# Last MLP of a hybrid decoder trunk: low parts of the weights made by an accumulating DMA onto the negated high parts, where VectorE subtracted

## The chip, the core and the metric

The kernel runs on one core of one Trainium2 chip. The time is device microseconds (us) for one execution of the whole program; a figure for a kernel is the median of several runs. The engines are named as in the profile: PE (TensorE matmuls), PEld (its weight loads), DVE (VectorE), ACT (ScalarE), POOL (GpSimd), SP (SyncE, which here only issues DMAs).

## What is computed

Two decoder layers on 528 tokens (16 learned meta tokens and 512 real ones) of width 1024, all in float32. Layer 0 is an mLSTM group beside an RG-LRU group, layer 1 is differential attention, and after each comes an MLP:

```python
def _sq_relu_mlp(hn, w1, w2):
    a = jax.nn.relu(hn @ w1)          # w1: 1024 x 4096
    return (a * a) @ w2               # w2: 4096 x 1024
...
        h = h + _sq_relu_mlp(_rmsnorm(h, norm_mlp[layer]), mlp_w1[layer], mlp_w2[layer])
    h = _rmsnorm(h, norm_final)
    return h[:, N_META:, :]
```

The change concerns the second of these MLPs, the last stage of the program.

## The kernel before

**Split products.** Matmuls run in float32r. To keep float32 accuracy every operand is split in two: a high part, which is the float32r rounding of the value, and a low part, which is the value minus its high part. A product is then three matmuls: high x high, high x low, low x high. For a weight tile `raw` the high part `wh` is made by a copy with conversion on ACT (L169) and the low part `wl = raw - wh` by a subtraction, usually on DVE (L117, the helper `sub`, called from L177).

**Units.** All weights are cut into 225 units of 128x1024 float32 (512 KB), used in a fixed order. `emit_load` (L150 to L179) prepares one unit: SP issues the load of `raw` (L162), ACT makes `wh`, DVE or POOL makes `wl`. `get_w` (L203) is called where a unit is used and first emits loads up to two units ahead. `unit_mm` (L210) then runs one unit: eight blocks k, and in each the three matmuls `wh`x high, `wh`x low, `wl`x high (L220). In the last MLP a matmul has 512 columns, so a unit is 24 matmuls, and `wl` is first read by the third of them.

**Buffers.** `raw` has two buffers (pool `wr`), `wh` and `wl` three each (pool `wp`). So the load of unit i+2 has to wait until everything that reads `raw` of unit i is done, and the copy that makes `wh` of unit i has to wait until PE has finished with unit i-3. The last eight units (indices 217 to 224) have eight buffers of their own for `wh` and `wl` (tag `wf`), and so are prepared ahead of their use.

**The last MLP.** It holds the unit indices 161 to 224: four quarters of 16 units, eight of w1 ("up") and eight of w2 ("down"). After an up unit DVE applies the relu and the norm's factor (L692), ACT squares (L694), ACT and DVE split the result (L120 and L117). After a down unit DVE adds the product to `h` (L705). The last eight units are the w2 of the fourth quarter; `final_quarter` takes them all at once, turned around so that tokens lie on the partitions, and goes through them eight times for four blocks of tokens: for the first block with k outermost, so unit 224 is needed last. The final norm and the output follow.

**Who makes the low parts.** A set `POOL_L` gives eight unit indices to POOL, 161 and 164 among them in the last MLP; all other low parts there are DVE's. Units 129 to 160 were split earlier in the program and are only loaded.

**Order.** Instructions of each engine stand in a fixed order, made by a scheduler from the order in the code and from priorities: what stands under `soon()` (the copy and the subtraction of a unit among it) is drawn forward.

Of the kernel before, what the change touches and what calls it, by code (L numbers as in the profile page):

```python
# [10 lines left out]
F32 = mybir.dt.float32  # L11
F32R = mybir.dt.float32r
AF = mybir.ActivationFunctionType
ALU = mybir.AluOpType
# [39 lines left out]
POOL_OPS = "Mm"  # L54

POOL_L = {5, 33, 43, 44, 52, 126, 161, 164}
N_S = 31

AHEAD = range(129, 161)
# [23 lines left out]
def trunk(tc, hT, wu, wri, pk, lv, rope, gf, out, probe=None):  # L83
    nc = tc.nc
# [6 lines left out]
    with ctx:  # L91
# [14 lines left out]
        def sc(name, dt=F32, w=T):  # L106

            return big.tile([P, T], dt, tag="s", name=name, bufs=N_S)

# [6 lines left out]
        def sub(eng, o, a, b):  # L116
            eng.tensor_tensor(out=o, in0=a, in1=b, op=ALU.subtract)  # L117
# [19 lines left out]
        def soon():  # L137
            return tc.high_priority(offset=BOOST)
# [12 lines left out]
        def emit_load():  # L151
            i = state["next"]
            u = seq[i]
            if i in AHEAD:
                wh, wl = (wp.tile([P, 1024], F32R, tag="w" + p, name=f"w{p}{i}") for p in "hl")
                for w, part in zip((wh, wl), parts[i - AHEAD[0]]):
                    nc.sync.dma_start(out=w.bitcast(F32), in_=part)
                ready.append((wh, wl))
                state["next"] += 1
                return  # L160
            raw = wr.tile([P, 1024], F32, tag="raw", name=f"raw{i}")
            nc.sync.dma_start(out=raw, in_=wu[u])  # L162
            if u >= N_UNIT - 8:
                wh, wl = (wp.tile([P, 1024], F32R, tag="wf" + p, name=f"w{p}{i}", bufs=8) for p in "hl")
            else:
                wh = wp.tile([P, 1024], F32R, tag="wh", name=f"wh{i}")
                wl = None if u == U_GATE else wp.tile([P, 1024], F32R, tag="wl", name=f"wl{i}")
            with soon():
                nc.scalar.copy(wh, raw)  # L169
                eng = nc.gpsimd if i in POOL_L else nc.vector  # L170
                if u == U_GATE:

                    hi, r = (a.rearrange("p (k c) -> p k c", k=KB) for a in (wh, raw))
                    sub(eng, hi[:, :, 64:100], r[:, :, 0:36], hi[:, :, 0:36].bitcast(F32))
                else:
                    sub(eng, wl, raw, wh.bitcast(F32))
            ready.append((wh, wl))  # L177
            state["next"] += 1
# [21 lines left out]
        def get_w(u):  # L200
            while state["next"] <= min(state["use"] + 2, len(seq) - 1):
                emit_load()
            assert seq[state["use"]] == u  # L203
            state["use"] += 1
            return ready.pop(0)
# [100 lines left out]

        h0 = big.tile([P, KB, T], F32, tag="h", name="h0")
        emit_load()
        for k in range(KB):
            nc.sync.dma_start(out=h0[:, k, :], in_=hT[:, k, :])  # L310
            if k == LOAD1:
                emit_load()
# [781 lines left out]
```

## Time and profile before

| | before |
|---|---|
| median of 3 runs | 1462.95 us (1461.53 to 1465.24) |
| the profiled execution, its own time | 1463.24 us |
| its span, first to last instruction | 1461.4 us |
| PE busy | 1437.9 us, 98% of the span |
| DVE busy | 814.5 us, 56% |
| ACT busy | 650.8 us, 45% |
| POOL busy | 214.0 us, 15% |
| granted TensorE clock | 0.999 |

The profile is of one execution. Its times are counted from the span's start. The views used below are: the page's summary of engines and its slices; busy time by stretch; groups of instructions by line; the table of waits (who waited for whom, total, times, longest); the list of DMA issues with sizes and the time from issue to landing; and the list of instructions in order of time, in which a row has the start, the duration, the engine, the line, the operation and its tiles, and in brackets how long the engine had been idle and what released it.

### The profile page before, as it was taken

How to read it: one execution, taken by the hardware profiler on the slowest of the kernel's cores; microseconds unless marked ns; L12 is line 12 of the kernel's file. 1: busy time of each engine (PE TensorE's matmuls, PEld its weight loads, DVE VectorE, ACT ScalarE, POOL GpSimd, SP SyncE). 2: the span in 40 equal slices, each digit the busy share in tenths (PEclk: the TensorE clock that was granted, in tenths of full speed). 3: DMA queues.
4: the chain of work that ended last, by engine and by line, in shares of the span. 5: the costliest groups of instructions: out<-in, count | busy, mean ns of one | idle time of the engine just before them, and what ended most of it. 6: DMA issues, size and time to landing. Idle time of an engine off the chain costs nothing. (4 is left out here: it accounts for less than half of the span.)

```text
span 1461.4 us, 24650 instructions
## 1 busy us (share of the span) xinstructions
PE 1437.9 (98%) x9970; PEld 1338.6 (92%) x9970; DVE 814.5 (56%) x1423; ACT 650.8 (45%) x1154; POOL 214.0 (15%) x286
## 2 busy tenths in 40 slices
PE   8999999999999999999999999999999999999998
PEld 8999999999999999999999998989887888888886
DVE  6867754667544545545445568777755344343452
ACT  6454743647334424334334536565644223142342
POOL 4000001010012231322314511101031000000001
PEclk9999999999999999999999999999999999999999
DMA  7332224231223685857857875555332332333331
GB/s 255 98 116 80 89 72 133 60 101 59 88 87 102 217 272 175 266 183 234 283 180 245 297 230 156 170 158 181 124 116 88 100 91 97 98 90 101 89 126 46
DMA packets 70046, 210.11 MB, mean 144 GB/s; under 512 B 13066, under 2 KB 14615, under 8 KB 69932
## 3 DMA queue, kind: packets, MB, share of 16 engines
q1 hardware_dynamic: 53996, 157.15, 34.4%
q0 software_dynamic: 15360, 50.34, 10.4%
q8 instruction: 78, 1.28, 0.4%
q10 hardware_dynamic: 576, 1.05, 0.2%
q14 instruction: 36, 0.29, 0.1%
HBM read 162.11 MB, written 35.71 MB: 135 GB/s over the span
## 5 line engine op out<-in xcount | busy, mean ns | idle before, releaser
L169 ACT CAST wh<-raw 128x1024 fp32r<-128x1024 f32 x193 | 202.6, 1050 | 503.7 <-PE mm L220 402.8
L117 DVE TENSOR_TENSOR wl<-raw,wh 128x1024 fp32r<-128x1024 f32 x184 | 227.1, 1235 | 66.9 <-ACT wh L169 66.5
L705 DVE TENSOR_TENSOR h<-mm,h 128x264 f32<-128x264 f32 (+1 forms) x88 | 41.2, 498 | 109.8 <-PE mm L220 109.8
L117 DVE TENSOR_TENSOR ral<-ra,rah 128x512 fp32r<-128x512 f32 x64 | 43.7, 688 | 56.4 <-ACT rah L120 56.4
L120 ACT CAST rah<-ra 128x512 fp32r<-128x512 f32 x64 | 39.5, 617 | 69.3 <-DMA ra<-wu 69.1
L692 DVE SCALAR_TENSOR_TENSOR rt<-mm,mrstd 128x264 f32<-128x264 f32 x64 | 24.7, 428 | 76.7 <-PE mm L220 76.7
L692 DVE SCALAR_TENSOR_TENSOR rt<-mm,nrstd 128x512 f32<-128x512 f32 x32 | 22.1, 692 | 79.2 <-PE mm L220 79.1
L273 POOL TENSOR_TENSOR nsq<-nsq 128x528 f32<-128x528 f32 (+1 forms) x28 | 46.2, 1652 | 93.1 <-ACT nsq L271 87.8
L982 POOL TENSOR_TENSOR zg<-z,gfr 128x512 f32<-128x512 f32 x4 | 5.2, 1296 | 342.0 <-DVE z L980 336.2
L785 POOL TENSOR_TENSOR qr<-qr,tb 128x512 f32<-128x512 f32 (+1 forms) x16 | 24.6, 1536 | 166.5 <-DVE qs L784 159.1
L117 POOL TENSOR_TENSOR wl<-raw,wh 128x1024 fp32r<-128x1024 f32 x8 | 19.2, 2403 | 201.6 <-ACT wh L169 120.4
L853 ACT ACTIVATE e<-psc,mx 128x264 f32<-128x264 f32 (+3 forms) x80 | 38.2, 482 | 9.1 <-DVE mx L846 8.1
L846 DVE TENSOR_REDUCE mx<-psc 128x1 f32<-128x264 f32 (+3 forms) x80 | 33.2, 430 | 15.5 <-PE psc L844 7.8
L694 ACT ACTIVATE rt<-rt 128x528 f32<-128x528 f32 (+1 forms) x64 | 40.6, 636 | 2.8 <-DVE rt L692 2.8
L197 POOL DMA_DIRECT2D ra<-wu x64 | 34.7, 547 | 2.9 <-issue 2.9
L663 DVE TENSOR_TENSOR h<-mm,h 128x264 f32<-128x264 f32 x32 | 12.2, 426 | 38.0 <-PE mm L220 38.0
L120 ACT CAST rh<-qr 128x512 fp32r<-128x512 f32 (+1 forms) x16 | 10.0, 627 | 51.2 <-DVE qr L787 48.2
L365 POOL TENSOR_SCALAR_AFFINE_SELECT cb<-cb 128x128 f32<-128x128 f32 (+2 forms) x20 | 7.7, 397 | 166.3 <-DMA cb<-crow 166.1
L886 ACT CAST pp<-pt 128x128 fp32r<-128x128 f32 (+2 forms) x64 | 21.0, 342 | 16.4 <-PE pt L874 14.4
L220 PE MATMUL mm<-ax0h,wh 128*128 128x264 f32 x98 | 22.0, 297 | 6.3 <-ACT ax0h L262 6.3
L840 PE MATMUL psc<-st,st 128*128 128x264 f32 (+3 forms) x80 | 26.4, 331 | 1.3 <-ACT e L853 0.9
L117 DVE TENSOR_TENSOR pp<-pt,pp 128x128 fp32r<-128x128 f32 (+2 forms) x64 | 23.8, 382 | 3.6 <-ACT pp L886 3.5
(866 smaller groups left out, 4908.7 us busy)
## 6 DMA issues: line engine op xcount, KB each, us to landing
raw<-wu SPq DMA_DIRECT2D x193, 512.0 KB
ra<-wu POOLq DMA_DIRECT2D x64, 256.0 KB, 5.0
h<-hT SPq DMA_DIRECT2D x16, 264.0 KB
st<-rh SPq DMA_DIRECT2D x32, 132.0 KB
kz<-rl SPq DMA_DIRECT2D x16, 132.0 KB
st<-rh SPq DMA_DIRECT2D x16, 128.0 KB
st<-rl SPq DMA_DIRECT2D x16, 128.0 KB
cb<-crow SPq DMA_DIRECT2D x4, 264.0 KB
```

The source lines that it names most:

```text
L117: eng.tensor_tensor(out=o, in0=a, in1=b, op=ALU.subtract)
L120: nc.scalar.copy(hl[0][:, sl], src)
L169: nc.scalar.copy(wh, raw)
L197: nc.gpsimd.dma_start(out=raw, in_=wu[seq[i]][:, c])
L273: nc.gpsimd.tensor_tensor(out=fin[0][:, lo:], in0=fin[0][:, lo:], in1=sq[:, lo:], op=ALU.add)
L692: nc.vector.scalar_tensor_tensor(out=t[:, tk], in0=p, scalar=0.0, in1=rs[:, tk], op0=ALU.max, op1=ALU.mult)
L694: nc.scalar.activation(out=t[:, lo:], in_=t[:, lo:], func=AF.Square)
L705: nc.vector.tensor_tensor(out=h[:, c, tk], in0=p, in1=h[:, c, tk], op=ALU.add)
L785: pool_or_dve("mM"[w]).tensor_tensor(out=raw[:, lo:], in0=raw[:, lo:], in1=tb[0][:, lo:], op=ALU.mult)
L840: nc.tensor.matmul(d[:, :m], qS[c][:, qs], kS[c][:, s0:s0 + m], start=True, stop=False)
L846: nc.vector.tensor_reduce(out=mx[:, 2 * c + r:2 * c + r + 1], in_=d[:, :m], axis=AX.X, op=ALU.max, negate=True)
L853: nc.scalar.activation(out=e[:, s0:s0 + m], in_=d[:, :m], func=AF.Exp, bias=mx[:, 2 * c:2 * c + 1], accum_out=ss[:, c + 2 * r:c + 2 * r + 1])
```

## The change

For the unit indices 165 to 216, 52 units of the last MLP, the low part is made in another way. ACT, which has just written `wh`, writes `-wh` into the `wl` tile (a second ACT pass over 128x1024), and then POOL issues a DMA that reads `raw` and adds it to what stands in `wl`. The subtraction on DVE is left out for these units. Units 161 and 164 stay with POOL, 162 and 163 with DVE, and the last eight, 217 to 224, with DVE. The numbers are the same, since `raw + (-wh)` is `raw - wh`.

```diff
 POOL_L = {5, 33, 43, 44, 52, 126, 161, 164}
+
+DMA_L = range(165, 217)
 N_S = 31
...
             with soon():
                 nc.scalar.copy(wh, raw)
+                if i in DMA_L:
+
+                    nc.scalar.activation(out=wl, in_=wh.bitcast(F32), func=AF.Copy, scale=-1.0)
+                    nc.gpsimd.dma_start(out=wl.bitcast(F32), in_=raw, accum_op=ALU.add)
                 eng = nc.gpsimd if i in POOL_L else nc.vector
                 if u == U_GATE:
...
-                else:
+                elif i not in DMA_L:
                     sub(eng, wl, raw, wh.bitcast(F32))
```

The line numbers of the changed kernel are higher by 2 at the helpers (L117 becomes L119, L120 becomes L122, L169 becomes L171) and by 6 behind `emit_load` (L694 becomes L700); the new lines are L174 (the negation) and L175 (the DMA).

On ACT, in the first up quarter of the last MLP, these rows stood before (a copy of a weight unit, the square and the copy of an activation):

```order
L169 CAST wh_13543<-raw_13541 128x1024
L694 ACTIVATE rt<-rt 128x512
L120 CAST a3h<-rt 128x512
L169 CAST wh_13581<-raw_13579 128x1024
L694 ACTIVATE rt<-rt 128x512
L120 CAST a4h<-rt 128x512
```

and these stand there now:

```order
L171 CAST wh_13545<-raw_13543 128x1024
L700 ACTIVATE rt<-rt 128x512
L174 ACTIVATE wl_13546<-wh_13545 128x1024
L122 CAST a3h<-rt 128x512
L171 CAST wh_13584<-raw_13582 128x1024
L700 ACTIVATE rt<-rt 128x512
L174 ACTIVATE wl_13585<-wh_13584 128x1024
L122 CAST a4h<-rt 128x512
```

The negation stands behind the square of an activation, not straight behind the copy that it reads; 28 of the 52 negations stand so. The other 24, in the down units, follow their copy directly:

```order
L171 CAST wh_13734<-raw_13732 128x1024
L174 ACTIVATE wl_13735<-wh_13734 128x1024
L171 CAST wh_13767<-raw_13765 128x1024
```

On POOL nothing stood between the low part of unit 164 and the four multiplications of the output; now the 52 DMAs stand there in a row, of which these are the first:

```order
L119 TENSOR_TENSOR wl_13430<-raw_13427,wh_13429 128x1024
L175 DMA wl_13468<-raw_13465 128x1024
L175 DMA wl_13507<-raw_13504 128x1024
L175 DMA wl_13546<-raw_13543 128x1024
```

On DVE the 52 subtractions are gone and the rest keeps its order. On SP the order is unchanged. On PE only a few transposes of the final quarter move (six of the eight that turn the second block of `h` now stand ahead of the first block's last `wl` matmuls).

## Prediction

> **What bounds the kernel now.** I read the summary first, then busy time by stretch over the last MLP, then the waits there, and last the instructions in order of time around one unit.
>
> ```profile
> PE 1437.9 (98%) x9970; PEld 1338.6 (92%) x9970; DVE 814.5 (56%) x1423; ACT 650.8 (45%) x1154; POOL 214.0 (15%) x286
> ...
> 1186.00:1231.00 45.00, 45.00 (x197) 36.59 (x196) 20.57 (x24) 17.19 (x24) 0.00 (x0) 1.00 0.29 94
> 1231.00:1275.00 44.00, 44.00 (x192) 35.61 (x191) 15.46 (x18) 8.87 (x9) 0.00 (x0) 1.00 0.32 96
> ```
>
> The stretches are an up and a down half of a quarter; the columns are length, then busy time of PE, PEld, DVE, ACT and POOL, the clock and the share of the DMA engines in use. PE is busy from end to end, DVE under half of the time. So what the change takes off is not what sets the time. The waits between 1050 us and the end say the same:
>
> ```profile
> ACT wh L169 <- PE mm L220: 198.4, 52, 4.5
> PE mm L220 <- DVE nx6l L263: 2.1, 1, 2.1
> PE mm L220 <- DVE nx7l L263: 0.7, 1, 0.7
> ```
>
> PE never waits for a low part of a weight; its two waits, 2.8 us, are for the stage's input. ACT waits for PE to give a `wh` buffer free. This is one up unit in order of time, first ACT's rows and DVE's subtraction, then SP's load and the matmuls of the unit that is being prepared:
>
> ```profile
> 1201.52 1.05 ACT L169 CAST wh<-raw 128x1024 fp32r<-128x1024 f32 x1 [3.30 <-PE mm L220]
> 1202.48 0.63 ACT L694 ACTIVATE rt<-rt 128x512 f32<-128x512 f32 x1
> 1202.61 1.23 DVE L117 TENSOR_TENSOR wl<-raw,wh 128x1024 fp32r<-128x1024 f32 x1 [0.16 <-ACT wh L169]
> 1203.14 0.62 ACT L120 CAST a2h<-rt 128x512 fp32r<-128x512 f32 x1
> 1203.86 0.33 SPq L162 DMA_DIRECT2D raw<-wu  x1
> ...
> 1207.06 1.06 ACT L169 CAST wh<-raw 128x1024 fp32r<-128x1024 f32 x1 [3.30 <-PE mm L220]
> ...
> 1213.08 0.40 PE L220 MATMUL mm<-nx0h,wl 128*128 128x512 f32 x1
> ```
>
> A unit takes 1207.06 - 1201.52 = 5.54 us. The low part begun at 1201.52 is ready at 1203.84, and PE asks for it at 1213.08: 9.2 us of cover. SP issues the next load 0.02 us after the subtraction, because that frees a `raw` buffer; only two exist, so one buffer's round must fit into 2 x 5.54 = 11.08 us.
>
> **What goes.** 52 subtractions of 1.23 us leave DVE, 64 us of its work. All of it ran beside PE and nothing on PE waited for it, so this term is 0. A gain of any size would need PE waits that aren't there.
>
> **What comes on ACT and POOL.** 52 negations of 128x1024. The nearest row is the copy of the same shape, 1.05 us: 55 us on ACT, which has 17.19 of 45 us in use, so as work it is covered. As latency it counts, since the DMA cannot start before it. In a down unit copy and negation run back to back: two such passes took 2.00 us (the row at 1390.12 below). In an up unit the square stands between: the negation starts where `a2h` did, at 1203.14, and ends at 1204.19, 2.67 us after the copy's start. POOL's issue of a DMA costs it half a microsecond (the rows below), on an engine that did nothing here. Its queue is in order: a DMA waiting for its negation holds up only the next DMAs and, at the end, the four output multiplications, which are needed later.
>
> **What the DMA takes.** No row shows an accumulating DMA. The nearest are plain DMAs from POOL, one alone and several together, and SP's loads of 512 KB:
>
> ```profile
> 491.77 0.54 POOL L187 DMA_DIRECT2D part130h<-rah  x1 [7.58 <-ACT rah L120]
> ...
> part130h<-rah POOLq DMA_DIRECT2D x1, 256.0 KB, 2.6
> ...
> q0 software_dynamic: 467, 1.52, 65.1%
> q1 hardware_dynamic: 167, 0.62, 32.5%
> ...
> part130h<-rah POOLq DMA_DIRECT2D x1, 256.0 KB, 5.1
> ```
>
> Alone, 256 KB land 2.6 us after the issue; between 493 and 500 us, where the two queues together hold 97.6% of the DMA engines, they take 5.1. For 512 KB the end of the program has rows: loads that ACT waits for.
>
> ```profile
> 1390.12 2.00 ACT L169 CAST wh<-raw 128x1024 fp32r<-128x1024 f32 x2 [3.30 <-PE mm L220]
> 1392.46 0.33 SPq L162 DMA_DIRECT2D raw<-wu  x1
> 1396.31 1.05 ACT L169 CAST wh<-raw 128x1024 fp32r<-128x1024 f32 x1 [3.00 <-DMA raw<-wu]
> ...
> 1410.67 0.33 SPq L162 DMA_DIRECT2D raw<-wu  x1
> 1414.18 1.05 ACT L169 CAST wh<-raw 128x1024 fp32r<-128x1024 f32 x1 [1.77 <-DMA raw<-wu]
> 1415.26 1.23 DVE L117 TENSOR_TENSOR wl<-raw,wh 128x1024 fp32r<-128x1024 f32 x1 [2.08 <-ACT wh L169]
> ...
> 1406.78 1.03 PE L954 MATMUL pht<-ident,h 128*128 128x128 f32 x8
> ...
> 1417.81 0.39 PE L973 MATMUL mf<-wl,a7h 128*128 128x512 f32 x1
> ```
>
> A load takes 1396.31 - 1392.46 = 3.85 us or 1414.18 - 1410.67 = 3.51 us, say L = 3.7. So 256 KB more cost 3.7 - 2.6 = 1.1 us. An accumulating DMA reads two tiles of 512 KB and writes one. Its low end is a plain 512 KB transfer, 3.7 us; its high end is two passes of 512 KB in company, which at 5.1 us for 256 KB might be 10.2. I take one more reading pass on top of the plain transfer, 3.7 + 2.2 = 5.9 us (A), near the low end, because a load leaves the engines idle for two thirds of the time (share 0.32).
>
> **The round of a raw buffer.** Load, copy and negation, DMA, and about 0.1 us of handing over. Down: 3.7 + 2.00 + 5.9 + 0.1 = 11.70; up: 3.7 + 2.67 + 5.9 + 0.1 = 12.37. Both are over 11.08, and as a round serves two units, PE would be slowed by 0.31 us in a down unit and 0.645 in an up unit: 24 x 0.31 + 28 x 0.645 = 7.4 + 18.1 = 25.5 us. First the cover is used up: the low part is now ready 2.67 + 0.1 + 5.9 = 8.7 us after the copy's start, and PE asks 11.56 us after it, so 2.9 us are free. Then there is company. A load alone uses 0.32 x 5.54 = 1.8 us of the DMA engines per unit, an accumulate perhaps twice that, together 5.4 of the 6 us, and one buffer's load falls beside the other's accumulate. Full company cost 5.1 - 2.6 = 2.5 us per transfer; for the two of a round that is 0 to 5.0. I take 0.8 a round, 0.4 a unit: 52 x 0.4 = 20.8 us.
>
> **The end.** Units 217 to 224 are still subtracted on DVE, but their loads wait for buffers that the last accumulates hold. Before, unit 224's low part was done at 1415.26 + 1.23 = 1416.49 and needed at 1417.81: only 1.3 us to spare. Now say unit 216's accumulate lands at W. The load of 218 starts there; its copy starts at W + 3.85; 220, 222 and 224 follow at three steps of (1414.18 - 1396.31) / 3 = 5.96 us, so 224's low part is done at W + 3.85 + 17.9 + 2.3 = W + 24.0. PE runs unit 216's third matmul at W, ends the unit 22 matmuls or 5.1 us later, begins the final quarter with eight transposes (at 1406.78 before) and asks for that low part 1417.81 - 1406.78 = 11.0 us behind its end: W + 16.1. It waits 7.9 us, of which the six transposes that now stand ahead fill 0.7: 7.2 us.
>
> The sum: 25.5 - 2.9 + 20.8 + 7.2 = 50.6 us. The profiled execution took 1463.24 us, 0.3 above the median, so its own time serves as base: 1514 us.
>
> **The rivals.**
>
> *The round fits.* If A is at most 4.9 us in company, the up round is 4.9 + 3.7 + 2.67 + 0.1 = 11.37 and the down round 10.70: what an up half loses (8 x 0.15 = 1.2 us) the cover holds and the down half gives back. PE then never waits inside the quarters; only the end is left. W is 1390.12 + 2.67 + 0.1 + A = 1397.8 at A = 4.9, 224's low part is done at 1421.8 against 1417.81, less 0.7: 3.3 us. With a plain transfer's 3.7 it is 2.1. So 1465 to 1467 us, which isn't slower by the 0.3% (4.4 us) that a measurement of this kernel can tell from no change. For it speaks the 2.6 us of a DMA alone; against it that the load is certain to fall beside an accumulate. The Trainium skill, "DMA: Bandwidth & Descriptors", section "Anatomy of one DMA — SWDGE (gpsimd) path", fits such a DMA as 2.0 us plus its bytes at 436 GB/s. For the 256 KB row that gives 2.6 us, as the trace has it; for two reads of 512 KB it gives an estimate of 4.4 us, by which the round fits. No row here shows whether the second read counts so. Chance 0.15.
>
> *The accumulate is slow.* The adding itself, or company, makes A about 8 us: rounds of 13.8 and 14.47, 1.36 us a down unit and 1.70 an up unit, 32.6 + 47.6 = 80 us, cover of 0.8 off, 7 at the end: 1550 us. At the high end of 10.2 it is 59 + 78 + 1.4 + 7 = 145 us, 1609. From A of about 8.8 the cover is gone from the first unit on. For it speaks the doubling to 5.1 us in company, against it that the DMA engines have room. Chance 0.26.
>
> *DVE's relief shows.* 64 us less on DVE could only help where PE waits for DVE, and the two waits of 2.8 us in this stage lie ahead of unit 165. 1460 us at best; chance 0.02.
>
> **How the numbers follow.** The forecast, rounds over 11.08 us with A between 5 and 7 in company, has 0.57 and spans about 1475 to 1550. Below the range I leave the faster case and a little of the fitting one, above it the slowest accumulates, 0.07: 1466 to 1600. Faster 0.02; same 0.14, the fitting case; slower 0.84.
>
> **What would show it.** In the changed profile: PE waits for `wl` from POOL's DMA in every unit, ACT's copies no longer wait for PE but for the DMA of `raw`, the interval between copies grows to about 6.3 us in the down halves and 6.6 in the up halves, the issue-to-landing time of the new DMA stands near 6 us (5 fits the first rival, 8 and more the second), and unit 224's wait shows at the first block of the final quarter. I am wrong if copies still come every 5.54 us, or if SP's loads start on time while PE waits for something else.

## The result, and the profile after

The changed kernel takes 1511.78 us (median of 4 runs, 1510.31 to 1513.22) against 1463.75 us of the kernel before on the same chip (4 runs): ratio 1.0329, 95% interval 1.0312 to 1.0347. It is slower by 48 us. The forecast was 1514.

The summary of engines of the changed kernel and its DMA row, the busy tenths of the DMA engines in 40 slices; below it the same row of the kernel before:

```profile
span 1508.5 us, 24812 instructions
PE 1457.0 (97%) x9970; PEld 1345.5 (89%) x9970; DVE 750.8 (50%) x1371; ACT 700.3 (46%) x1206; POOL 258.8 (17%) x338
...
DMA  7332223231224757858679655554347777777741
...
DMA  7332224231223685857857875555332332333331
```

DVE lost its 64 us, ACT's busy time grew by 49.5, and the DMA engines' busy tenths in the last MLP went from 3 to 7. Busy time alone would not show the loss: PE is still at 97%. The stretches show it (columns as before: length, PE, PEld, DVE, ACT, POOL, clock, DMA share, GB/s). The first row is the kernel before, the other two are the changed kernel:

```profile
1200.00:1400.00 200.00, 200.00 (x867) 162.48 (x866) 83.65 (x94) 62.87 (x78) 0.00 (x0) 1.00 0.32 98
...
1200.00:1400.00 200.00, 183.67 (x758) 145.59 (x757) 32.11 (x48) 82.00 (x96) 27.54 (x32) 0.97 0.73 167
...
1100.00:1444.50 344.50, 320.52 (x1328) 253.89 (x1328) 59.23 (x88) 142.75 (x171) 47.41 (x53) 0.97 0.71 161
```

In 200 us of the last MLP PE ran 758 matmuls, where the kernel before ran 867. This is the table of waits of the changed kernel, first from 1050 us to the end, then PE's rows between 1100 and 1456 us:

```profile
POOL wl L175 <- ACT wl L174: 239.6, 46, 10.1
ACT wh L171 <- DMA raw<-wu: 197.7, 42, 8.4
...
PE mm L226 <- DMA wl<-raw: 13.3, 12, 2.0
PE mm L226 <- ACT a7h L122: 9.5, 3, 4.1
PE mf L979 <- ACT wh L171: 1.8, 2, 1.5
```

Before, ACT's copy waited for PE (198.4 us); now it waits for the load of `raw`, for the same total. And SP's load waits for the accumulate, 315.2 us in 52 waits, in the queue's own table:

```profile
SPq L164 <- DMA wl<-raw: 315.2, 52, 11.9
```

Before, SP waited for DVE's subtraction, 290.2 us in 60 waits, and PE lost nothing by that. So the sum of these waits does not measure the loss; the length of a round does.

One round of a raw buffer in an up half, in order of time: POOL's rows, then SP's, then ACT's.

```profile
1242.29 0.86 POOL L175 DMA_DIRECT2D wl<-raw  x1 [8.73 <-ACT wl L174]
1245.74 0.86 POOL L175 DMA_DIRECT2D wl<-raw  x1 [2.59 <-ACT wl L174]
1255.32 0.86 POOL L175 DMA_DIRECT2D wl<-raw  x1 [8.72 <-ACT wl L174]
...
1246.86 0.33 SPq L164 DMA_DIRECT2D raw<-wu  x1
...
1252.51 1.04 ACT L171 CAST wh<-raw 128x1024 fp32r<-128x1024 f32 x1 [6.55 <-DMA raw<-wu]
1253.46 0.62 ACT L700 ACTIVATE rt<-rt 128x512 f32<-128x512 f32 x1
1253.99 1.04 ACT L174 ACTIVATE wl<-wh 128x1024 fp32r<-128x1024 f32 x1
1254.93 0.60 ACT L122 CAST a7h<-rt 128x512 fp32r<-128x512 f32 x1
```

The accumulate issued at 1242.29 lands 4.5 us later, as the list of DMA issues for that moment says; the one at 1245.74 takes 5.5:

```profile
wl<-raw POOLq DMA_DIRECT2D x1, 512.0 KB, 4.5
...
wl<-raw POOLq DMA_DIRECT2D x1, 512.0 KB, 5.5
```

At 1246.86, the moment of that landing, SP issues the next load into the same buffer. ACT can copy it at 1252.51, 5.65 us later, where a load alone took 3.5 to 3.85 in the kernel before: most of the second accumulate runs beside it. Copy, square and negation end at 1255.03, and POOL issues this buffer's next accumulate at 1255.32. The round is 13.03 us, and it serves two units that PE could do in 11.08.

### The profile page after: what moved, and what is told of

Its sections match the earlier page's. It is cut to its first block, busy times and chain, and to the rows that moved or that the text cites. A ratio compares the mean times of both kernels' runs of the same rounds, so it can differ in the third digit from the quotient of the medians.

```text
span 1508.5 us, 24812 instructions
## 1 busy us (share of the span) xinstructions
PE 1457.0 (97%) x9970; PEld 1345.5 (89%) x9970; DVE 750.8 (50%) x1371; ACT 700.3 (46%) x1206; POOL 258.8 (17%) x338
## 5 line engine op out<-in xcount | busy, mean ns | idle before, releaser
L171 ACT CAST wh<-raw 128x1024 fp32r<-128x1024 f32 x193 | 202.4, 1049 | 488.9 <-DMA raw<-wu 221.9
L119 DVE TENSOR_TENSOR wl<-raw,wh 128x1024 fp32r<-128x1024 f32 x132 | 163.5, 1239 | 67.2 <-ACT wh L171 66.6
L175 POOL DMA_DIRECT2D wl<-raw x52 | 44.8, 861 | 286.1 <-ACT wl L174 239.6
L119 DVE TENSOR_TENSOR ral<-ra,rah 128x512 fp32r<-128x512 f32 x64 | 43.8, 688 | 55.4 <-ACT rah L122 55.3
L122 ACT CAST rah<-ra 128x512 fp32r<-128x512 f32 x64 | 39.5, 618 | 68.0 <-DMA ra<-wu 67.8
L174 ACT ACTIVATE wl<-wh 128x1024 fp32r<-128x1024 f32 x52 | 54.6, 1050 | 0.8
L119 POOL TENSOR_TENSOR wl<-raw,wh 128x1024 fp32r<-128x1024 f32 x8 | 19.6, 2447 | 201.0 <-ACT wh L171 160.6
L700 ACT ACTIVATE rt<-rt 128x528 f32<-128x528 f32 (+1 forms) x64 | 40.7, 635 | 12.7 <-DVE rt L698 12.6
L122 ACT CAST rh<-qr 128x512 fp32r<-128x512 f32 (+1 forms) x16 | 10.0, 627 | 51.2 <-DVE qr L793 48.2
L226 PE MATMUL mm<-a7h,wh 128*128 128x264 f32 (+1 forms) x88 | 23.1, 322 | 9.5 <-ACT a7h L122 9.5
L669 DVE TENSOR_TENSOR h<-mm,h 128x264 f32<-128x264 f32 x32 | 12.4, 428 | 39.3 <-PE mm L226 39.3
```

Source lines behind the costliest of these rows:

```text
L122: nc.scalar.copy(hl[0][:, sl], src)
L174: nc.scalar.activation(out=wl, in_=wh.bitcast(F32), func=AF.Copy, scale=-1.0)
L175: nc.gpsimd.dma_start(out=wl.bitcast(F32), in_=raw, accum_op=ALU.add)
L226: nc.tensor.matmul(p[:, :m], w[:, c], xx[:, s:s + m], start=(k == 0 and j == 0), stop=(k == KB - 1 and j == len(terms) - 1))
L700: nc.scalar.activation(out=t[:, lo:], in_=t[:, lo:], func=AF.Square)
```

## The experiments

Each kernel ran on one chip with the kernel before; a ratio is to that kernel, whose median was 1464.75 us beside the first four runs and 1464.46 us beside the last four. Theory: a raw buffer is held through the accumulate, and with two buffers the round is too long. Rivals: load and accumulate together exceed the DMA engines; the extra pass on ACT costs; the waits are separate and add up.

**A third set of raw data.** Every third of the 52 units loads into two scratch tiles, and its copy and accumulate come in halves.

```diff
...
+            if i in DMA_L and i % 3 == 2:
+                halves_ = [(c, sc(f"raw{i}")[:, :512]) for c in (slice(0, 512), slice(512, 1024))]
+                for c, r_ in halves_:
+                    nc.sync.dma_start(out=r_, in_=wu[u][:, c])
+            else:
...
+                for c, r_ in halves_:
+                    nc.scalar.copy(wh[:, c], r_)
...
+                    for c, r_ in halves_:
+                        nc.gpsimd.dma_start(out=wl[:, c].bitcast(F32), in_=r_, accum_op=ALU.add)
```

> The changed kernel, but every third of the 52 units gets its raw data in two scratch tiles of 256 KB each instead of one of the two raw buffers, so that three sets of raw data can be under way; its load, copy and accumulating DMA come in two halves, and nothing else changes. Theory (the round of a raw buffer binds: load, copy, negation and accumulate must fit into two units, 11.08 us): with three buffers a round may take 16.6 us, the measured rounds of 11.8 to 13.0 fit, ACT's copies wait for PE again, PE's waits for low parts inside the quarters go, and only the end is late: 1464 to 1472 us. First rival (the DMA engines' throughput binds, since load and accumulate share them): more buffers give no more throughput, still 1500 us or more. Second rival (the extra pass on ACT and its place in ACT's queue): still 1505 to 1515 us.

Measured 1474.93 us, ratio 1.0076 (1.0056 to 1.0097). The list of DMA issues:

```profile
wl<-raw POOLq DMA_DIRECT2D x35, 512.0 KB, 6.1
wl<-raw POOLq DMA_DIRECT2D x34, 256.0 KB, 6.0
```

37 of the 48 us are gone, although an accumulate now takes longer in the median than in the changed kernel (6.1 us against 5.4). So it is not its duration alone that PE pays for; with more buffers a longer one costs less. The time is 3 us over what the theory allowed. That the transfers of these units come in halves was not tried by itself.

**A plain DMA in place of the accumulating one.**

```diff
-                    nc.gpsimd.dma_start(out=wl.bitcast(F32), in_=raw, accum_op=ALU.add)
+                    nc.gpsimd.dma_start(out=wl.bitcast(F32), in_=raw)
```

> The changed kernel with a plain DMA in place of the accumulating one: raw is copied over the negated high part, so the low parts are left out of the numbers and stand for the whole weight; the queue, the issue, the waits and the size stay. Theory: what hurts is that any DMA holds the raw buffer before it can be loaded again; a plain one takes 3.7 us where the accumulate took 4.5 alone, the round is 0.8 us or more shorter and the loss is 5 to 25 us of the 48. Rival (the accumulate costs no more than a copy, only its issue and company count): 1505 to 1515 us. Rival (all of the cost is the adding): within 0.3% of the kernel before.

Measured 1466.17 us, ratio 1.0014 (1.0004 to 1.0023). The rows of one such DMA, alone, in order of time and in the list of issues:

```profile
1260.60 0.53 POOL L175 DMA_DIRECT2D wl<-raw  x1 [7.31 <-DMA raw<-wu]
...
wl<-raw POOLq DMA_DIRECT2D x1, 512.0 KB, 2.8
```

The theory expected a loss of 5 to 25 us and missed: the loss is 2. Its figure came from a plain DMA of 3.7 us; it takes 2.8 alone and 3.1 in the median of the 52. At 2.8 the up round is 2.8 + 3.7 + 2.67 + 0.1 = 9.3 us and fits with room. By itself this run would also suit the rival that all the cost is the adding. The run with every other unit and the last but one speak against that: there the adding is done, and nearly nothing is lost.

**The negation alone.** DVE adds `raw` to the negated tile.

```diff
-                    nc.gpsimd.dma_start(out=wl.bitcast(F32), in_=raw, accum_op=ALU.add)
+                    nc.vector.tensor_tensor(out=wl, in0=raw, in1=wl.bitcast(F32), op=ALU.add)
```

> Half of the change: ACT negates the high part into the low part's tile, but DVE adds raw to it, where the changed kernel uses the DMA. Theory: the ACT pass is covered (the low part is ready about 3.9 us after the copy's start where 11.5 are allowed, and the raw buffer's round is 3.7 + 2.7 + 1.2 + 0.1 = 7.7 of 11.08 us): 1460 to 1468 us, no change against the kernel before; the end may cost 1 us or 2. Rival (the ACT pass or its place in the queue costs): 1480 us or more.

Measured 1465.6 us, ratio 1.001 (1.0001 to 1.002). But for some 1.5 us the ACT pass is covered, as in the prediction.

**Every other unit.** The odd units keep the accumulating DMA, the even ones are done as in the run above.

```diff
+                    if i % 2:
+                        nc.gpsimd.dma_start(out=wl.bitcast(F32), in_=raw, accum_op=ALU.add)
+                    else:
+                        nc.vector.tensor_tensor(out=wl, in0=raw, in1=wl.bitcast(F32), op=ALU.add)
```

> The changed kernel, but only the odd ones of the 52 units get the accumulating DMA; the even ones are negated on ACT too, and DVE adds raw. So one raw buffer has all the accumulates, 26, and never meets another accumulate. Theory (a round is too long because an accumulate meets the other buffer's accumulate and load): alone the round is 4.5 + 3.7 + 2.7 + 0.1 = 11.0 us in an up half and 10.3 in a down half, which fits 11.08; company with the other buffer's load may add 0.5 to 1 us in places: 1464 to 1475 us. Rival (each accumulate costs its own share, 48 / 52 = 0.9 us): 26 x 0.9 = 24, 1488 us.

Measured 1466.72 us, ratio 1.0016 (1.0007 to 1.0026).

```profile
wl<-raw POOLq DMA_DIRECT2D x26, 512.0 KB, 4.5
```

26 accumulates cost 2 us, not 24, and part of the 2 is the negation of the run above. Without another accumulate beside them they land in 4.5 us in the median and 5.3 at most, and a round of 11.0 just fits. The loss isn't a price per accumulate; it begins where the round passes two units.

**The last up half back on DVE.**

```diff
-DMA_L = range(165, 217)
+DMA_L = range(165, 209)
```

> The changed kernel, but only units 165 to 208 get the accumulating DMA; the last up half (209 to 216) goes back to DVE. Theory (part of the loss is the end: the loads of the last eight units come late, because the last accumulates hold the raw buffers): the final quarter's PE waits of 5.1 us and the half clock behind them go, with the drift of eight units (13.0 - 11.08 over two units, 0.96 each, 7.7 us): 12 to 16 us less than the changed kernel, about 1497 us. Rival (no effect of the end, each unit an equal share of 48 us): 8 x 0.92 = 7 us less, 1505 us.

Measured 1495.39 us, ratio 1.021 (1.0191 to 1.0228): 0.0119 of 1464, or 17 us less than the changed kernel, for 8 of 52 units, where 12 to 16 were expected. In its table of waits the final quarter no longer waits for a weight. The expectation put 7.7 us of it down to the rounds of the eight units; the rest, some 9 us, is the end, a cost of its own.

**a7 first.** On ACT the copy of the weight unit behind an up half is queued behind the square and the copy of a7 (three places).

```diff
+            hold = state.pop("hold", None)
-            with soon():
+            with soon(), (tc.issue_after(hold.ins) if hold else nullcontext()):
                 nc.scalar.copy(wh, raw)
...
+                    if last and j == 7 and q < 3:
+                        state["hold"] = last_a
```

> The changed kernel with one order changed on ACT, three times: the copy of a weight unit that stood ahead of the square and the copy of a7 (the last activation of an up half) now stands behind them, so that PE no longer waits for a7 while ACT waits for raw data. Theory (the rounds of the raw buffers set the pace, and the wait for a7 only stands where a later wait for a low part would stand): nearly no gain, 0 to 5 us less than the changed kernel. Rival (the waits add up, the place in ACT's queue is a cost of its own): 9.5 us of waits and some 5 us of half clock behind them less, 1497 us.

Measured 1509.13 us, ratio 1.03 (1.0279 to 1.032): some 4 us less than the changed kernel by the ratios, as the theory allowed, and the two intervals overlap. PE's waits, from 1065 us on:

```profile
PE mm L228 <- DMA wl<-raw: 26.3, 21, 2.7
PE mf L983 <- ACT wh L173: 3.5, 3, 1.6
```

The waits for a7 are gone, and those for the low part went from 13.3 to 26.3 us. They moved; the rounds set the pace.

**More raw data.** As the first run, with every second unit in scratch tiles.

```diff
-            if i in DMA_L and i % 3 == 2:
+            if i in DMA_L and i % 2:
```

> As the run with every third unit's raw data in scratch tiles, which left 11 us of the 48, but every second unit's: more than three sets of raw data can be under way. Theory (what was left is still rounds of the two real raw buffers, held by accumulates in company): the two real buffers then serve one unit in two and have 22 us for a round: 1464 to 1470 us. Rival (what was left is the DMA engines' limit or the end): the same as with every third, 1473 to 1477 us.

Measured 1469.11 us, ratio 1.0032 (1.0018 to 1.0045).

```profile
1200.00:1400.00 200.00, 199.35 (x863) 161.84 (x863) 40.35 (x58) 99.63 (x132) 46.27 (x54) 1.00 0.81 189
...
ACT wh L179 <- PE mm L235: 99.7, 38, 4.6
```

All 52 accumulates are done, the DMA engines are at 0.81, more than in the changed kernel, and PE runs 863 matmuls in 200 us. ACT's copies wait for PE again, 99.7 us, against 11.3 for the load. The remaining 5 us were not explained.

**The traffic alone.** The kernel before, and for each of the 52 units two accumulating DMAs of 256 KB onto scratch tiles.

```diff
+            if i in range(165, 217):
+                for xk in state["nx"][:2]:
+                    extra = sc("extra")[:, :512]
+                    nc.gpsimd.memset(extra, 0.0)
+                    nc.gpsimd.dma_start(out=extra, in_=xk[0][:, NM:].bitcast(F32), accum_op=ALU.add)
...
+            state["nx"] = mx
```

> The kernel before, with its subtractions on DVE, and for each of the 52 units two extra accumulating DMAs of 256 KB from POOL, from a finished activation tile onto a scratch tile that POOL has set to zero; their result is used by nothing. The traffic is that of the changed kernel, but it holds no raw buffer. Theory (holding the raw buffer is the cause, not traffic): a load in company takes up to 5.7 us, a round 5.7 + 1.05 + 1.23 + 0.1 = 8.1 of 11.08 us: 1462 to 1468 us. Rival (load and accumulate together exceed the DMA engines): 1490 us or more.

Measured 1464.6 us, ratio 0.9996 (0.9986 to 1.0005).

```profile
1200.00:1400.00 200.00, 200.00 (x867) 162.62 (x866) 84.04 (x94) 62.88 (x78) 76.80 (x112) 1.00 0.74 176
...
DMA  2237999999999994332328999999999523333334
...
extra<-nx0h POOLq DMA_DIRECT2D x30, 256.0 KB, 14.0
```

The DMA engines are as busy as in the changed kernel (0.74 against 0.73) and PE loses nothing. They are not evenly busy: the row of tenths (40 slices of the same 200 us) shows 90% or more for about 50 us at a time, twice, and two to four tenths between. And the extra DMAs do fall behind: 30 pairs in a stretch in which PE does 36 units. So this run has the changed kernel's traffic per time, not more. That the DMA engines can serve PE's full pace is shown by the run before it.

## Why the prediction was right

**Direction and mechanism.** The step that decided was that a raw buffer is held until the DMA has landed, that two buffers allow 11.08 us for a round, and that the new round is longer. The runs with more raw data (the accumulates stay, the buffers grow, the loss goes) and the one with the traffic alone (the buffers are free, the traffic stays, no loss) show it from both sides. The relief of DVE was worth nothing, as put, and the negation alone cost some 1.5 us (1.001).

**The sizes.** The final quarter begins 37.7 us later than before (its transposes at 1444.48 against 1406.78) and takes 9.4 us more (64.0 against 54.6 to the span's end), 47.1 together. The prediction had 43.4 for the quarters and 7.2 for the end.

```profile
1444.48 1.03 PE L960 MATMUL pht<-ident,h 128*128 128x128 f32 x8
```

Between the first and the last accumulate (1110.4 and 1432.6, 51 steps) a unit takes 6.32 us; the sum's rounds, company included, were 12.5 and 13.2 us, 6.4 a unit. But that agreement holds two errors against each other, and to that extent the close time is luck. The accumulate alone was put at 5.9 us and takes 4.5, the shortest of the 52: the plain transfer in it takes 2.8 and not 3.7, and the adding 1.7 and not 2.2:

```profile
DMA to landing us min/median/max: 4.5/5.4/7.8
```

Company was put at 0.8 us a round and is 2.1 in the round shown (13.03 against 4.5 + 3.7 + 2.67 + 0.1 = 10.97). There nearly all of it falls on the load, but not everywhere. The first 14 accumulates come one by one, 5.5 to 6.8 us apart, and take 6.0 us in the median; the other 38 come in pairs, as above, and take 5.2. In a round of the first kind (accumulates issued at 1135.22 and 1147.86) the accumulate takes 5.9 us and the load 3.9, and of the 1.7 us of company most falls on the accumulate. By this sum the round would just have fitted if each transfer had run alone; the run with every other unit comes nearest to that, and loses 2 us.

The rival that it fits had the right A, with its estimate of 4.4 us from the Trainium skill, "DMA: Bandwidth & Descriptors", section "Anatomy of one DMA — SWDGE (gpsimd) path"; the trace agrees for an accumulate alone (4.5) and not in company (5.4 in the median). That the second read counts as the first is not shown by this: for the plain 512 KB the same fit of the Trainium skill gives an estimate of 3.2 us, and 2.8 was measured. What that rival lacked was the price of company.

**The signs.** As put, ACT's copies wait for the load of `raw`, and the interval between copies grew: a round takes 13.0 us in the up half shown, and 12.4, 11.9 and 11.8 by POOL's next issues, in the down half behind it, which is 6.5 and about 6.0 us a unit (forecast 6.6 and 6.3). The new DMA's time, forecast near 6 us, is 5.4 in the median. Two signs were wrong. PE was to wait for `wl` in every unit; it has 12 such waits in 52 units. And unit 224 was to be waited for in the final quarter. These rows are, in order of time, ACT's copy of unit 218, PE's first wait there, for unit 220, ACT's copy of unit 224, and PE's first reading of 224's low part:

```profile
1444.12 1.04 ACT L171 CAST wh<-raw 128x1024 fp32r<-128x1024 f32 x1
...
1451.14 0.50 PE L979 MATMUL mf<-wh,a3h 128*128 128x512 f32 x1 [1.46 <-ACT wh L171]
...
1463.40 1.04 ACT L171 CAST wh<-raw 128x1024 fp32r<-128x1024 f32 x1 [3.51 <-DMA raw<-wu]
...
1465.92 0.71 PE L979 MATMUL mf<-wl,a7h 128*128 128x512 f32 x2
```

The last accumulate lands at 1438.2 (W in the prediction) and DVE finishes 224's low part at 1465.7: W + 27.5, not W + 24.0. Some 2 us of that come from the copy of 218, which stands on ACT behind the square and the copy of a5 and starts at W + 5.9, not W + 3.85. PE would have asked for 224's low part at 1444.5 + 11.0 = 1455.5. It came 10.2 us later; less the 0.7 that the six transposes fill, that is 9.5, near the 9.4 by which the quarter is longer. But PE spent that time earlier, in waits of 5.1 us in all for units 220 to 222 and in matmuls at a lower clock, and had no wait left at 224. So the mechanism of the end was right, its size 2 us short, and the place of the wait wrong.

**What was not foreseen.** PE waited 9.5 us for a7 (the last activation of an up half), which stood on ACT behind a copy that waited for raw data; the prediction had looked at what is queued behind POOL's wait and not behind ACT's. It cost little on top, since the wait stands in place of a later one (the run with a7 first gained some 4 us). And PE's clock fell after some of the waits. These are PE's rows after the longest wait for a7, and the stretch around them:

```profile
1255.59 0.50 PE L226 MATMUL mm<-a7h,wh 128*128 128x512 f32 x1 [4.08 <-ACT a7h L122]
1256.38 0.80 PE L226 MATMUL mm<-a7l,wh 128*128 128x512 f32 x1 [0.29 <-DVE a7l L119]
1256.98 0.63 PE L226 MATMUL mm<-a7h,wl 128*128 128x512 f32 x1
...
1259.83 0.40 PE L226 MATMUL mm<-a2h,wh 128*128 128x512 f32 x1
...
1255.60:1262.00 6.40, 6.11 (x19) 4.71 (x20) 1.38 (x2) 1.94 (x2) 1.44 (x2) 0.73 0.88 162
```

A matmul takes 0.63 us instead of 0.39 for some three microseconds after a wait of 4.08, and the clock granted over 6.4 us is 0.73. Over the span it is 0.989 against 0.999. Of the 47 us, 28 are more idle time on PE (51.5 against 23.5) and 19 are more busy time (1457.0 against 1437.9). Which part of the latter would have become waits at full clock wasn't separated. In the final quarter the slow matmuls filled time in which PE would else have waited for unit 224, whose low part was done only at 1465.7.

## What to carry to other kernels

Work moved from a compute engine to a DMA is not only a matter of busy time: count how long each buffer that the DMA reads is held, add the load that refills it, and compare the round with what the buffers allow. With two buffers a step of 1.2 us became one of 4.5 to 5.4 (7.8 at most), and in company either this step or the refill grew. Where the source buffer is the limit, more buffers take most of the loss away (1475 us here with every third unit's data apart, 1469 with every second). Nothing was won in any run, since PE in this stage never waited for a low part that DVE made.

## What the runs showed of the hardware that was not expected

- A 512 KB DMA from POOL from one tile to another took 2.8 us alone (the run with the plain DMA), with accumulation 4.5; its issue on POOL took 0.53 us plain and 0.86 us accumulating.
- The price of company can fall on either party. In the pair shown the first accumulate kept its 4.5 us, the second took 5.5, and the load beside it 5.65 us instead of 3.5 to 3.85; in the round where accumulates came one by one, the accumulate took 5.9 us and the load 3.9.
- Accumulates took longer where more were in flight: 6.1 us in the median with a third set of raw data, and 14.0 for 256 KB where nothing waited for them.
- PE's clock halved after some waits. The Trainium skill, "TensorE: Matmul & The Clock Gate", section "What's actually happening", describes a halved clock judged over windows of about 3.4 us; the trace agrees on the length (0.27 of 6.4 us lost is 3.5 us at half clock). That section of the Trainium skill names an idle window of that length as the condition; here a wait of 1.91 us, ending at 1334.02, was enough (granted clock 0.50 from 1334.8 to 1338.1), while two of 1.85 and 1.64 us, ending at 1233.84 and 1246.85, passed without it (1.00 from 1229 to 1255). So the length of the wait alone did not decide.
